# Four feed-forward gate/up groups as seven block products each, with the weight sums made on VectorE and by accumulating DMAs

## The chip, the cores and the metric

The kernel runs on one core of a Trainium2 chip. The metric is the device time of one execution in microseconds (us). Before the change it is 411.26 us, the median of 3 runs (410.68 to 411.28).

The engines are named as the profile names them: PE (TensorE, the matrix engine, with PEld its weight loads), DVE (VectorE), ACT (ScalarE), POOL (GpSimd) and SP (SyncE, which here only issues DMAs). A name with a q (SPq, POOLq) is the sequencer of that engine.

## The reference

One decoder layer on 256 tokens of width 1024, in float32: a token mixer (block-sparse attention and retention), a cross-attention into 256 memory rows, and a gated feed-forward part. The change lies in the last of these:

```python
h = rms_norm(x, g_pre_ffn[l])
gu = h @ w_gate_up[l]                                  # 1024 -> 2 * 2816
f = (jax.nn.silu(gu[..., :D_FF]) * gu[..., D_FF:]) @ w_down[l]
x = x + rms_norm(f, g_post_ffn[l])
```

`rms_norm(x, g)` scales each token's row by the inverse root of its mean square and each column by the gain `g`. `D_FF` is 2816, 22 tiles of 128 columns.

## The kernel before

All weights stand in DRAM as 130 blocks of 128 x 1024 floats, in the order of their use. Each goes through three stages.

- **Load.** SP's queue loads block q into one of 5 raw tiles (`load_weight`, L128), as soon as a raw tile is free.
- **Split.** `split_weight` makes two halves of it in one of 9 `hl` tiles (`RING`): ACT copies the block, rounded to the matmul's float32r type, into the high half (L136), and DVE subtracts that from the raw tile into the low half (L138). For 12 blocks of the feed-forward part (`POOL_LOW`) POOL does the subtraction.
- **Use.** A product of two split operands is three matmuls: high by high, high by low, low by high. The dropped term is low by low.

What PE does is a list of steps, built once; a step works on one block. Three of its forms matter here.

- **col** (L858 to L860): 128 tokens are stationary, 512 weight columns move; six matmuls of 512 columns for a block and a token half.
- **row** (L872, L874): a 128 x 128 weight tile is stationary and the tokens move. One matmul takes the 256 tokens' high and low halves side by side (512 columns) and a second one the high half against the weights' low half (256 columns). Eight such pairs make one tile of 128 gate or up columns for all tokens, already transposed.
- **down** (L892 to L894): as col, with the gated result as stationary operand, into four PSUM accumulators that stay open to the end.

The feed-forward part has six groups of gate and up columns. Group 0 (512 gate and 512 up columns) is in col form, first for tokens 0 to 127, then for 128 to 255, so that its 8 blocks are held through two passes; its result is transposed on PE (`c_f`, L501). Groups 1 to 4 (four gate and four up tiles each) and group 5 (two and two) are in row form; ACT, DVE and ACT again add the two halves of each accumulator, scale by the token's inverse root (a row `R_x2`, since tokens lie along the free axis), apply silu and multiply (L513 to L530). The down steps of a group stand behind the row steps of the next one.

The order of everything else is fixed by hand: what follows a step is a generator that is resumed a given number of steps later (the table `WAIT`), and splits are placed one per step, when the `hl` tile nine blocks back has been used. All instructions of an engine run in the order in which they were written down, and wait there for the tiles they need.

Ahead of the feed-forward part, `post_and_pre("cross", t)` adds the normalised output of the cross-attention to the 128 tokens of half t (L412), takes the mean square, and transposes x_sb on PE (`xt_cross`, L426); ACT and DVE scale it by the gain and split it into `x2T`. The inverse root is applied later, to gate and up.

Of the kernel before, what the change touches and what calls it, by code (L numbers as in the profile page):

```python
# [38 lines left out]
POOL_LOW = range(74, 122, 4)  # L39
# [5 lines left out]
def tile_hybrid_layer(  # L45
# [77 lines left out]
    raws, hls = {}, {}  # L123

    def load_weight(q):
        if q < NQ:
            raws[q] = rawp.tile([P, D], F32, tag="raw", name=f"raw{q}")
            nc.sync.dma_start(raws[q], weights[q])  # L128

    def split_weight(q, parts=1):  # L130
        raw = raws.pop(q)
        h = hlp.tile([P, 2, D], F32R, tag="hl", name=f"hl{q}")
        w = D // parts
        for i in range(parts):
            n = slice(i * w, (i + 1) * w)
            nc.scalar.activation(h[:, 0, n], raw[:, n], AF.Copy)  # L136
            eng = nc.gpsimd if q in POOL_LOW else nc.vector
            eng.tensor_tensor(out=h[:, 1, n], in0=raw[:, n], in1=h[:, 0, n].bitcast(F32), op=ALU.subtract)  # L138
# [25 lines left out]
    def split4(name, k0, t, c, n=4):  # L164
        dst = T[name][:, 0] if name == "fT" else T[name]
# [3 lines left out]
        emitted.update((name, k, t) for k in range(k0, k0 + n))  # L169
# [244 lines left out]
    def post_and_pre(stage, t, g, dst_name, key):  # L414
# [6 lines left out]
        dst = T[dst_name]  # L421
        for half in range(2):
# [72 lines left out]
    def ffn_up(t, acc):  # L495
        f = tmp2k(f"f0_{t}")
        nc.vector.scalar_tensor_tensor(f, acc, rstd[f"x2{t}"][:, 0:1], T[f"sg0_{t}"], op0=ALU.mult, op1=ALU.mult)
        yield WAIT[f"f0_{t}"]
        c = accC(f"c_f0_{t}")
        for i in range(4):  # L500
            nc.tensor.transpose(c[:, i, :], f[:, i * P:(i + 1) * P], ident)  # L501
        split4("fT", 0, t, c)

    def ffn_gate(t, acc):
        sg = tmp2k(f"sg0_{t}")
        nc.scalar.activation(sg, acc, AF.Silu, scale=rstd[f"x2{t}"][:, 0:1])
        T[f"sg0_{t}"] = sg

    def ffn_gate_T(i, acc):
# [6 lines left out]
        nc.vector.tensor_tensor(out=sg, in0=sg, in1=T["R_x2"], op=ALU.mult)  # L516
        yield WAIT["g_silu"]
        nc.scalar.activation(sg, sg, AF.Silu)  # L518
        yield WAIT["g_row"]
# [109 lines left out]

    def col_steps(order, tiles, done, st, skip=0):  # L630
# [4 lines left out]
        base = nq[0]  # L635
        nq[0] += len(order)
# [62 lines left out]
    def down_steps(js, tiles):
        blocks = [(j, kk) for j in js for kk in range(4 if j < 5 else 2)]  # L700
        base = nq[0]
        nq[0] += len(blocks)
        for ts in tiles:
            for i, (j, kk) in enumerate(blocks):
                for t in ts:
                    steps.append(("down", base + i, t, j, kk, (0, 1)))

    col_steps(plain([0, 1]), first_then, gu_first, "x2T")
    for j in range(1, 5):
        gu_steps(range(4 * j, 4 * j + 4))  # L710
        if j < 4:
            down_steps([j - 1], both)
    down_steps([3], both)
    gu_steps((20, 21))
    down_steps([4, 5], [(0,)])
    blocks_base = nq[0] - 6
    for half in range(2):
        for i in range(6):
# [299 lines left out]
```

## Time and profile before

| | us |
|---|---|
| median of the runs | 411.26 |
| span of the profiled execution, first to last instruction | 409.1 |
| PE busy | 401.2 |
| DVE busy | 290.9 |
| ACT busy | 237.5 |
| POOL busy | 42.5 |
| feed-forward groups' matmuls in row form, summed durations | 102.2 + 81.0 |

The mean granted clock of PE is 0.995 of full speed. Matmuls are pipelined, so their durations overlap and their sum says more than the time they take; the distance from the start of one to the start of the next is what they cost. DVE's and ACT's instructions overlap a little too, by less than 0.1 us.

The profiled execution's own time is its span, 409.1 us, and what lies around it: the median of the runs is 2.16 us above the span.

### The profile page before, as it was taken

Reading aid. Unit: us, or ns where it says so; the run is one execution under the profiler, and the core shown is the slowest. Engines: PE = TensorE matmul, PEld = TensorE weight load, DVE = VectorE, ACT = ScalarE, POOL = GpSimd, SP = SyncE. Lnnn points to the kernel's source line nnn. Section 1 sums busy time; section 2 is a strip of 40 time slices with the busy share of each in tenths; the row PEclk is TensorE's granted clock in tenths of the full one; section 3 lists DMA queues with packets and bytes.
Section 4 is the critical chain, followed back from the end, with each engine's and each line's share of the span. In section 5 each row is a group of like instructions: output and inputs, shape, how many; then the busy total and the mean of one; then the engine's idle time right before and its main releaser. Section 6 shows DMA issues by size and latency. Waiting matters only on the chain.

```text
span 409.1 us, 5760 instructions
## 1 busy us (share of the span) xinstructions
PE 401.2 (98%) x2114; PEld 336.9 (82%) x2114; DVE 290.9 (71%) x444; ACT 237.5 (58%) x438; POOL 42.5 (10%) x33
## 2 busy tenths in 40 slices
PE   8999999999999999999999999999999999999993
PEld 4888787888888888888888888888888888888882
DVE  4876975765889966678359577777878687777632
ACT  4887785945776763686158566374454545555411
POOL 0010100100010000000011031222222222200000
PEclk9999999999999999999999999999999999999997
DMA  7988654475656565147306756458457447456001
GB/s 264 410 346 286 229 187 167 147 259 181 208 184 199 190 211 166 49 158 256 105 14 209 265 183 205 154 172 291 123 189 256 155 154 269 143 154 207 1 27 75
DMA packets 21627, 76.17 MB, mean 186 GB/s; under 512 B 2400, under 2 KB 2656, under 8 KB 21600
## 3 DMA queue, kind: packets, MB, share of 16 engines
q1 hardware_dynamic: 21456, 75.56, 54.4%
q8 instruction: 16, 0.26, 0.3%
q10 hardware_dynamic: 144, 0.26, 0.2%
q14 instruction: 11, 0.09, 0.1%
HBM read 74.76 MB, written 1.05 MB: 185 GB/s over the span
## 4 chain that ended last, share of the span: by engine, by line
PE 94%; issue 2%; DMA 1%; ACT 0%; SPq 0%; DVE 0%; DVEq 0%; POOLq 0%; POOL 0%; ACTq 0%
PE acc L872 24%; PE acc L874 12%; PE acc L858 12%; PE acc L860 12%; PE acc L859 12%; PE down L892 4%; PE down L894 4%; PE down L893 4%; PE acc L845 2%; DMA raw<-in_weights_dram 1%; PE s_m L277 1%; PE o_m L306 1%; PE pt_m L256 1%; PE ro L359 0%; PE s_c L446 0%
## 5 line engine op out<-in xcount | busy, mean ns | idle before, releaser
L138 DVE TENSOR_TENSOR hl<-raw,hl 128x1024 fp32r<-128x1024 f32 (+1 forms) x120 | 147.2, 1251 | 41.2 <-ACT hl L136 36.4
L136 ACT ACTIVATE hl<-raw 128x1024 fp32r<-128x1024 f32 (+1 forms) x132 | 132.5, 1037 | 7.9 <-DMA raw<-in_weights_dram 6.2
L872 PE MATMUL acc<-x2T,hl 128*128 128x512 f32 x288 | 102.2, 399 | 0.0
L874 PE MATMUL acc<-x2T,hl 128*128 128x256 f32 x288 | 81.0, 281 | 0.0
L872 PEld LDWEIGHTS acc<-x2T,hl 128*128 128x128 f32 x288 | 54.2, 188 | 13.3
L874 PEld LDWEIGHTS acc<-x2T,hl 128*128 128x128 f32 x288 | 54.5, 189 | 0.2
L138 POOL TENSOR_TENSOR hl<-raw,hl 128x1024 fp32r<-128x1024 f32 x12 | 30.7, 2556 | 100.6 <-ACT hl L136 80.7
L892 PE MATMUL down<-hl,fT 128*128 128x512 f32 x88 | 34.3, 390 | 0.0
L893 PE MATMUL down<-hl,fT 128*128 128x512 f32 x88 | 34.3, 390 | 0.0
L894 PE MATMUL down<-hl,fT 128*128 128x512 f32 x88 | 34.3, 390 | 0.0
L858 PE MATMUL acc<-hl,xT 128*128 128x512 f32 x80 | 32.7, 409 | 0.0
L860 PE MATMUL acc<-hl,xT 128*128 128x512 f32 x80 | 31.4, 392 | 0.0
L859 PE MATMUL acc<-hl,xT 128*128 128x512 f32 x80 | 31.2, 390 | 0.0
L449 ACT ACTIVATE fT<-sg 128x256 fp32r<-128x256 f32 x18 | 7.5, 418 | 29.4 <-DVE sg L530 29.3
L872 PE MATMUL acc<-memT,hl 128*128 128x512 f32 x64 | 22.9, 400 | 0.0
L872 PE MATMUL acc<-x1T,hl 128*128 128x512 f32 x64 | 22.7, 399 | 0.0
L530 DVE TENSOR_TENSOR sg<-sg 128x256 f32<-128x256 f32 x18 | 20.1, 1118 | 0.6
L518 ACT ACTIVATE sg<-sg 128x256 f32<-128x256 f32 x18 | 7.5, 418 | 22.0 <-DVE sg L516 22.0
L894 PEld LDWEIGHTS down<-hl,fT 128*128 128x128 f32 x88 | 16.5, 188 | 3.5
L892 PEld LDWEIGHTS down<-hl,fT 128*128 128x128 f32 x88 | 16.5, 188 | 3.5
L893 PEld LDWEIGHTS down<-hl,fT 128*128 128x128 f32 x88 | 16.5, 188 | 3.3
L874 PE MATMUL acc<-x1T,hl 128*128 128x256 f32 x64 | 18.0, 281 | 0.0
(210 smaller groups left out, 724.8 us busy)
## 6 DMA issues: line engine op xcount, KB each, us to landing
raw<-in_weights_dram SPq DMA_DIRECT2D x129, 512.0 KB, 4.3
gpost<-in_gpost_dram SPq DMA_DIRECT2D x3, 512.0 KB, 5.2
x_sb<-in_x_dram SPq DMA_DIRECT2D x2, 512.0 KB, 6.9
memn<-in_mem_dram SPq DMA_DIRECT2D x2, 512.0 KB, 6.4
mr<-in_memT_dram SPq DMA_DIRECT2D x2, 512.0 KB, 5.1
out_dram<-x_sb SPq DMA_DIRECT2D x4, 256.0 KB, 2.0
xr<-in_gx_dram SPq DMA_DIRECT2D x1, 512.0 KB, 8.7
cst<-in_consts_dram SPq DMA_DIRECT2D x1, 512.0 KB, 7.6
```

Source lines behind the costliest of these rows:

```text
L136: nc.scalar.activation(h[:, 0, n], raw[:, n], AF.Copy)
L138: eng.tensor_tensor(out=h[:, 1, n], in0=raw[:, n], in1=h[:, 0, n].bitcast(F32), op=ALU.subtract)
L530: nc.vector.tensor_tensor(out=f, in0=f, in1=buf[:, 0:256], op=ALU.mult)
L845: nc.tensor.matmul(accs[(c, t)], T["xT"][:, hx, 2 * kp + kk, tok(t)], h[:, hw, :], start=begin, stop=False)
L858: nc.tensor.matmul(acc, xh, h[:, 0, kk, :], start=(first and kk == 0), stop=False)
L859: nc.tensor.matmul(acc, xh, h[:, 1, kk, :], start=False, stop=False)
L860: nc.tensor.matmul(acc, xl, h[:, 0, kk, :], start=False, stop=(last and kk == 1))
L872: nc.tensor.matmul(acc.rearrange("p (s m) -> p s m", s=2), hls[q][:, 0, n], T[st][:, :, k, :], start=(k == 0), stop=False, skip_group_chec ...
L874: nc.tensor.matmul(acc[:, 0:256], hls[q][:, 1, n], T[st][:, 0, k, :], start=False, stop=(k == 7), skip_group_check=True)
L892: nc.tensor.matmul(acc, fh, wh, start=first, stop=False, skip_group_check=True)
L893: nc.tensor.matmul(acc, fh, wl, start=False, stop=False, skip_group_check=True)
L894: nc.tensor.matmul(acc, fl, wh, start=False, stop=last, skip_group_check=True)
```

## The change

**Block products.** For groups 1 to 4, gate and up are computed together in col form as one product of 2 x 2 blocks: rows are the two token halves, the inner dimension is the two halves of the width, columns are 512 gate columns and 512 up columns. With A the tokens and B the weights, eight products of blocks are replaced by seven (`P1` to `P7`), each of 12 matmuls with 128 x 512 moving columns:

- P1 = A11 B11, P2 = A12 B21, P5 = S1 (B11 + B12), P6 = S2 (B11 + B12 + B22), P3 = S4 B22, P7 = S3 (B22 + B12), P4 = A22 (B11 + B12 + B21 + B22),
- with S1 = A21 - A22, S2 = S1 - A11, S3 = A11 - A21, S4 = S2 + A12.

P1, P6, P7 and P4 add up in one PSUM bank (`bA`), P5 and P3 in another (`bC`), P2 has a third (`bG`). Between the products ACT copies the bank's state (P1, P5, P1 + P6) and DVE combines (gate of half 0 = P1 + P2; up of half 0 = P5 + P3 less P1 + P6; up of half 1 = P5 less P1 + P6 + P7; gate of half 1 is the bank after P4).

**Sums of weights.** Raw tiles now serve several splits. DVE adds one raw tile to another in place (L195 of the new kernel; P6 and P4: 16 sums), and after the splits of P1 and of P3 a DMA on POOL's queue adds block B12 from DRAM onto the raw tile (L198; 16 DMAs). Each product has its own split: 14 per group where there were 8. There are 122 blocks loaded by SP. POOL no longer makes low halves. Raw tiles are 8 from the cross-attention on, and five idle buffers of other pools serve as raw tiles too.

**Tokens.** The inverse root and the gain are applied before the transposes (`y`), ACT keeps an unsplit copy (`af`), and DVE forms S1 to S4 and their low halves (`sh`, `sl`) once. The row `R_x2` goes. The gated result of groups 1 to 4 is token-major and is transposed on PE like that of group 0 (`ffn_mult`). Group 5 stays in row form and moves ahead into group 1. Down blocks are interleaved with the products (`ffn_plan`). The waits of steps around this part are set anew, and in the feed-forward part up to two splits are placed per step.

On PE, where group 1 begins: before, the pairs of the row form (`acc146` is a gate tile, `hl72` its split block);

```order
L860 MATMUL acc142_2319<-hl71_2198,x2T_1949 128x512
L872 MATMUL acc146_2361<-x2T_1949,hl72_2209 128x512
L874 MATMUL acc146_2361<-x2T_1949,hl72_2209 128x256
L872 MATMUL acc146_2361<-x2T_1949,hl72_2209 128x512
L874 MATMUL acc146_2361<-x2T_1949,hl72_2209 128x256
```

and now, between P5 (`bC1`) and P6 (`bA1`) of group 1, with the transposes of group 0's result:

```order
L1071 MATMUL bC1_2425<-hl77_2359,sh_2308 128x512
L1072 MATMUL bC1_2425<-hl77_2359,sh_2308 128x512
L1073 MATMUL bC1_2425<-hl77_2359,sl_2309 128x512
L1071 MATMUL bA1_2370<-hl80_2401,sh_2308 128x512
L1072 MATMUL bA1_2370<-hl80_2401,sh_2308 128x512
...
L1073 MATMUL bA1_2370<-hl80_2401,sl_2309 128x512
L622 MATMUL c_f0_1_2451<-cst_93,sg0_1_2326 128x128 x4
L1071 MATMUL bA1_2370<-hl81_2417,sh_2308 128x512
```

The pairs of 512 and 256 columns have become triples of 512; tile 80 is used ahead of 78 and 79, which belong to P3.

On DVE, at the same place, before:

```order
L497 SCALAR_TENSOR_TENSOR f0_0_2280<-acc134_2250,r_x20_2070,sg0_0_2220 128x512
L138 TENSOR_TENSOR hl73_2301<-raw73_2119,hl73_2301 128x1024
L138 TENSOR_TENSOR hl75_2326<-raw75_2184,hl75_2326 128x1024
L138 TENSOR_TENSOR hl76_2337<-raw76_2201,hl76_2337 128x1024
L138 TENSOR_TENSOR hl77_2348<-raw77_2212,hl77_2348 128x1024
L497 SCALAR_TENSOR_TENSOR f0_1_2359<-acc142_2319,r_x21_2196,sg0_1_2312 128x512
```

and now, from the split of P5's second block on (`hl77`; `raw72` and `raw73` are the two B11 blocks of group 1, `raw76` and `raw77` its B22 blocks):

```order
L184 TENSOR_TENSOR hl77_2359<-raw73_2071,hl77_2359 128x1024
L195 TENSOR_TENSOR raw72_1977<-raw72_1977,raw76_2122 128x1024
L618 TENSOR_TENSOR sg0_1_2326<-acc142_2334,sg0_1_2326 128x512
L184 TENSOR_TENSOR hl78_2377<-raw76_2122,hl78_2377 128x1024
L195 TENSOR_TENSOR raw73_2071<-raw73_2071,raw77_2151 128x1024
L184 TENSOR_TENSOR hl79_2397<-raw77_2151,hl79_2397 128x1024
L184 TENSOR_TENSOR hl80_2401<-raw72_1977,hl80_2401 128x1024
L230 TENSOR_TENSOR fT_2176<-c_f0_0_2410,fT_2176 128x4x128
L184 TENSOR_TENSOR hl81_2417<-raw73_2071,hl81_2417 128x1024
```

Ahead of these rows stand, new too, the splits 73 to 76 and, between 74 and 75, the eight instructions of 128 x 512 that form S1 to S4 and their low halves.

On POOL, before the first of the feed-forward part's low halves and now the first accumulating DMAs:

```order
L150 TENSOR_TENSOR r_x21_2196<-v_x21_2194,mhalf_99 128x1
L138 TENSOR_TENSOR hl74_2314<-raw74_2171,hl74_2314 128x1024
L138 TENSOR_TENSOR hl78_2377<-raw78_2304,hl78_2377 128x1024
L138 TENSOR_TENSOR hl82_2492<-raw82_2351,hl82_2492 128x1024
L138 TENSOR_TENSOR hl86_2601<-raw86_2469,hl86_2601 128x1024
```

```order
L210 TENSOR_TENSOR r_x21_2218<-v_x21_2216,mhalf_99 128x1
L198 DMA raw72_1977<-in_weights_dram 128x1024
L198 DMA raw73_2071<-in_weights_dram 128x1024
L198 DMA raw76_2122<-in_weights_dram 128x1024
L198 DMA raw77_2151<-in_weights_dram 128x1024
```

POOL's instructions on tiles have become DMAs on its queue; `raw73`, written by the second of them, is read again by the split `hl77` above.

The core of the diff:

```diff
 RING = 9
-RAW = 5
+RAW = 8
-POOL_LOW = range(74, 122, 4)
+PRODUCTS = {
+    "P1": ("A", "A11"), "P2": ("G", "A12"), "P5": ("C", "S1"), "P6": ("A", "S2"),
+    "P3": ("C", "S4"), "P7": ("A", "S3"), "P4": ("A", "A22"),
+}
+CHAIN = {
+    "P1": ("b11", None, "b12", ()), "P2": ("b21", None, None, ()), "P5": ("b11", None, None, ()),
+    "P3": ("b22", None, "b12", ()), "P6": ("b11", "b22", None, ()), "P4": ("b11", "b21", None, ("b11", "b21")),
+    "P7": ("b22", None, None, ("b22",)),
+}
...
+    pe = [(1, "P1 P2 P5 P6 r P3 r P1+ r P7 r P4 d"), (2, "P2 d P5 P6 d P3 d P1+ d P7 d P4"),
+          (3, "P2 d P5 P6 d P3 d P1+ d P7 d P4"), (4, "P2 d P5 P6 d P3 d d P7 d P4 d")]
+    prep = [(1, "P1 P2 P5 P3 P6 r r P1+ r P4 P7 r d"), (2, "P2 d P5 P3 P6 d d P1+ d P4 P7 d"),
+            (3, "P2 d P5 P3 P6 d d P1+ d P4 P7 d"), (4, "P2 d P5 P3 P6 d d P4 d P7 d d d d d d d")]
...
+    def split_weight(h, parts=1):
+
+        kind, q, add, more, frees = preps[h]
+        raw = raws[q][0]
+        split_raw(h, raw, parts)
+        while added[0] < min(len(preps), h + 1 + WAIT["ahead"]):
+            q, add = preps[added[0]][1:3]
+            if add is not None:
+                nc.vector.tensor_tensor(out=raws[q][0], in0=raws[q][0], in1=raws[add][0], op=ALU.add)
+            added[0] += 1
+        if more is not None:
+            nc.gpsimd.dma_start(raw, weights[more], accum_op=ALU.add)
+        for r in frees:
+            release(r)
...
+    def ffn_tokens(t, dst):
+        ys = []
+        for half in range(2):
+            n = slice(half * 512, (half + 1) * 512)
+            y = tmp2k(f"y{t}{half}")
+            nc.vector.scalar_tensor_tensor(y, x_sb[:, t, n], rstd[f"x2{t}"][:, 0:1], T["gpre"][:, n], op0=ALU.mult,
+                                           op1=ALU.mult)
+            ys.append(y)
...
+    def ffn_mult(j, t, up, wait):
+
+        f = T.pop(f"sg{j}_{t}")
+        nc.vector.tensor_tensor(out=f, in0=up, in1=f, op=ALU.mult)
+        yield wait
+        c = accC(f"c_f{j}_{t}")
+        for i in range(4):
+            nc.tensor.transpose(c[:, i, :], f[:, i * P:(i + 1) * P], ident)
+        split4("fT", 4 * j, t, c)
...
+        elif s[0] == "str":
+            _, q, j, prod, b = s
...
+            for kk in range(2):
+                ah, al = token_form(form, 2 * b + kk)
+                nc.tensor.matmul(acc, ah, h[:, 0, kk, :], start=first and kk == 0, stop=False, skip_group_check=True)
+                nc.tensor.matmul(acc, ah, h[:, 1, kk, :], start=False, stop=False, skip_group_check=True)
+                nc.tensor.matmul(acc, al, h[:, 0, kk, :], start=False, stop=b == 1 and kk == 1, skip_group_check=True)
...
-        if pending_split:
+        for n in range(2):
+            if not pending_split:
+                break
             q = pending_split[0]
-            paced = q <= 2 + WAIT["pace"] * 0.01 * i
-            free = q < RING or last_use[q - RING] + WAIT["lag"] <= i
-            if paced and free and (quiet or q - s[1] <= WAIT["low"]):
-                split_weight(pending_split.pop(0), 2 if q < 4 else 1)
+            if not all(last_use[h] + WAIT["lag"] <= i for h in range(q - RING + 1)):
+                break
+            if q < ffn_prep:
+                go = n == 0 and q <= 2 + WAIT["pace"] * 0.01 * i and (quiet or q - s[1] <= WAIT["low"])
+            else:
+                lead = first_use[q] - i
+                go = lead <= (WAIT["flow"] if n or not quiet else WAIT["flead"])
+            if not go:
+                break
+            split_weight(pending_split.pop(0), 2 if q < 4 else 1)
```

In `CHAIN` a product names the block it splits, the block that DVE adds to it first, the block that a DMA adds afterwards, and the blocks it frees. In the plan, a letter r stands for a row tile of group 5, d for a down block, and P1+ for P1 of the next group.

More of the change, by code (lines that the diff above doesn't have):

```diff
@@ L628, in tile_hybrid_layer, with plain_blocks @@
     nq = [0]
+    def plain_blocks(n):
+        h = len(preps)
+        for _ in range(n):
+            preps.append(("plain", nq[0], None, None, (nq[0],)))
+            loads.append(nq[0])
+            nq[0] += 1
+        return h
     def col_steps(order, tiles, done, st, skip=0):
@@ L649, in row_steps @@
         for i in tiles:
+            h = plain_blocks(1)
             for half in range(2):
-                steps.append(("row", nq[0], half, st, i, done))
-            nq[0] += 1
+                steps.append(("row", h, half, st, i, done))
     def plain(chunks):
@@ L688, in gu_first @@
         if c == 0:
-            ffn_gate(t, acc)
-        else:
-            spawn(ffn_up(t, acc))
+            sg = tmp2k(f"sg0_{t}")
+            nc.scalar.activation(sg, acc, AF.Silu)
+            T[f"sg0_{t}"] = sg
+        else:
+            spawn(ffn_mult(0, t, acc, WAIT[f"f0_{t}"]))
+    col_steps(plain([0, 1]), first_then, gu_first, "x2T")
+    pe_order, prep_order, load_order, extra = ffn_plan()
+    block = {k: nq[0] + n for n, k in enumerate(load_order + extra)}
+    loads.extend(range(nq[0], nq[0] + len(load_order)))
@@ L693, in gu_done @@
+    at = {}
+    ffn_prep = len(preps)
+    for item in prep_order:
+        at[item] = len(preps)
+        if item[0] in CHAIN:
+            src, add, more, frees = CHAIN[item[0]]
+            src, add, more = (n and block[(n, *item[1:])] for n in (src, add, more))
+            preps.append((item, src, add, more, tuple(block[(n, *item[1:])] for n in frees)))
+        else:
+            preps.append((item, block[item], None, None, (block[item],)))
     def gu_done(i, acc):
         return ffn_up_T(i - 100, acc) if i >= 100 else ffn_gate_T(i, acc)
-    def gu_steps(tiles):
-        row_steps([i + up for i in tiles for up in (0, 100)], gu_done, "x2T")
@@ L699, in down_steps @@
[L699 to L716, printed above, removed]
+    for item in pe_order:
+        if item[0] in CHAIN:
+            steps.append(("str", at[item], item[1], item[0], item[2]))
+        elif item[0] == "row":
+            for half in range(2):
+                steps.append(("row", at[item], half, "x2T", item[1], gu_done))
+        else:
+            for t in range(2):
+                steps.append(("down", at[item], t, item[1] // 4, item[1] % 4, (0, 1)))
@@ L717, in tile_hybrid_layer @@
+    tail = [(k, at[item]) for item in prep_order if item[0] == "down" and item not in pe_order for k in item[1:]]
+    for k, h in tail:
+        steps.append(("down", h, 0, k // 4, k % 4, (0, 1)))
     for half in range(2):
-        for i in range(6):
-            j, kk = (4, i) if i < 4 else (5, i - 4)
-            steps.append(("down", blocks_base + i, 1, j, kk, (half,)))
-    assert nq[0] == NQ, nq[0]
+        for k, h in tail:
+            steps.append(("down", h, 1, k // 4, k % 4, (half,)))
@@ L723, in tile_hybrid_layer, with raw_tile @@
     last_use = {s[1]: i for i, s in enumerate(steps)}
+    first_use = {s[1]: i for i, s in reversed(list(enumerate(steps)))}
     nc.vector.memset(junk[:, 0:512], 0.0)
     nc.gpsimd.memset(mhalf, -0.5)
-    raws[0] = rawp.tile([P, D], F32, tag="raw", name="raw0")
-    nc.scalar.dma_start(raws[0][:, 0:512], weights[0, :, 0:512])
+    def raw_tile():
+        q = loads.pop(0)
+        raw_free["raw"] -= 1
+        raws[q] = (rawp.tile([P, D], F32, tag="raw", name=f"raw{q}"), "raw")
+        return raws[q][0]
```

231 lines of the change are left out of this document (174 added, 57 removed), and 16 rows, old and new, of the table WAIT.

## The prediction

> **What bounds the kernel now.** I read the page's busy times and its chain of waits first, then the granted clock and engine loads by windows, then TensorE's (PE's) instructions one by one.
>
> ```profile
> span 409.1 us, 5760 instructions
> PE 401.2 (98%) x2114; PEld 336.9 (82%) x2114; DVE 290.9 (71%) x444; ACT 237.5 (58%) x438; POOL 42.5 (10%) x33
> PE 94%; issue 2%; DMA 1%; ACT 0%; SPq 0%; DVE 0%; DVEq 0%; POOLq 0%; POOL 0%; ACTq 0%
> ...
> 15.00:110.00 95.00, 95.00 (x519) 77.26 (x519) 70.72 (x110) 68.88 (x136) 5.14 (x6) 1.00 0.66 231
> ...
> 265.00:290.00 25.00, 25.00 (x131) 21.32 (x130) 20.14 (x25) 13.27 (x20) 7.81 (x3) 1.00 0.65 214
> 290.00:315.00 25.00, 25.00 (x129) 21.25 (x129) 18.83 (x26) 13.51 (x22) 5.41 (x2) 1.00 0.60 204
> ```
>
> The chain that ended last is PE for 94%, and no window between 15 and 390 us has idle time on PE (the first busy figure equals the window) at a granted clock of 1.00. So an instruction taken from PE shortens the run by its pitch, as long as its suppliers keep up. The nearest supplier is VectorE (DVE), which in the feed-forward windows works 20.1 and 18.8 us of 25.
>
> The mean durations on the page (399 ns for a 128x512 matmul) overlap. What counts is the distance from start to start:
>
> ```profile
> 261.63 0.40 PE L872 MATMUL acc<-x2T,hl 128*128 128x512 f32 x1
> 261.86 0.28 PE L874 MATMUL acc<-x2T,hl 128*128 128x256 f32 x1
> ...
> 263.75 0.39 PE L892 MATMUL down<-hl,fT 128*128 128x512 f32 x1
> ...
> 267.86 0.39 PE L892 MATMUL down<-hl,fT 128*128 128x512 f32 x1
> ```
>
> ```profile
> 242.04 0.48 PE L872 MATMUL acc<-x2T,hl 128*128 128x512 f32 x1
> 242.35 0.28 PE L874 MATMUL acc<-x2T,hl 128*128 128x256 f32 x1
> ```
>
> ```profile
> 241.84 0.44 PE c_f L501 x4
> ```
>
> The first two fences are the timeline of PE (start, duration), the third a piece of the chain (start, length). Six pairs L872+L874 take 263.75 - 261.63 = 2.12 us, 0.353 us a pair; the eighteen matmuls from 263.75 to 267.86 take 4.11 us, 0.228 us each. Four 128x128 transposes take 0.44 us.
>
> **The change on PE.** L872 and L874 are the weight-stationary form (a tile of 128 gate or up columns, eight pairs each); of the 36 feed-forward tiles in these groups 32 go:
>
> ```profile
> L872 PE MATMUL acc<-x2T,hl 128*128 128x512 f32 x288 | 102.2, 399 | 0.0
> L874 PE MATMUL acc<-x2T,hl 128*128 128x256 f32 x288 | 81.0, 281 | 0.0
> ```
>
> Removed: 256 pairs x 0.353 = 90.4 us, and the two transposes of the row norm with what follows them, 0.2. Added: 4 groups x 7 products x 12 matmuls of 512 columns = 336 x 0.228 = 76.6 us. Eight products a group in the new form would be 87.6 us, so 2.8 us come from leaving the pair form and 11.0 from the missing product. Added too: the gated result of each group is now token-major and is transposed, 32 transposes x 0.11 = 3.5 us, in 8 batches; the first matmul behind a batch holds PE 0.31 us instead of 0.23 (242.04 to 242.35), 0.6 in all. Down products (264 matmuls) and the first group stay. Net 90.6 - 76.6 - 3.5 - 0.6 = **9.9 us less PE**, if PE never waits.
>
> **The change on DVE.** Uncontended prices, and the pitch when splits follow each other:
>
> ```profile
> L138 DVE TENSOR_TENSOR hl<-raw,hl 128x1024 fp32r<-128x1024 f32 x22 | 26.2, 1221 | 4.2 <-ACT hl L136 4.2
> L248 DVE TENSOR_TENSOR p_m<-p_m,rs_m 128x1024 f32<-128x1024 f32 x3 | 3.7, 1225 | 0.1
> L405 DVE TENSOR_TENSOR cg_mix<-acc,gpost 128x512 f32<-128x512 f32 x4 | 2.7, 687 | 2.2 <-ACT junk L155 2.2
> L450 DVE TENSOR_TENSOR fT<-sg,fT 128x256 fp32r<-128x256 f32 x18 | 7.6, 422 | 3.9 <-ACT fT L449 3.9
> L136 ACT ACTIVATE hl<-raw 128x1024 fp32r<-128x1024 f32 x126 | 129.1, 1056 | 5.8 <-DMA raw<-in_weights_dram 4.2 <-PE acc L860 1.6
> ```
>
> ```profile
> 211.71 3.50 DVE L138 TENSOR_TENSOR hl<-raw,hl 128x1024 fp32r<-128x1024 f32 x3 [0.80 <-ACT hl L136]
> ```
>
> These are groups of instructions by line and shape (count, busy us and mean ns, idle us before them and its releaser; the first between 140 and 215 us, where POOL has no split), then a row of DVE's timeline. Pitch of a 128x1024 instruction: (3.50 - 1.22) / 2 = 1.14 us, 0.08 under its duration; the same taken off gives 0.61 for 512 columns and 0.34 for 256. An in-place weight sum has the shape of L248 (1.225), so 1.14 too. A middle group (from its P2 to the next P2) holds on DVE 19 splits, 4 sums and 7 instructions of 512: 23 x 1.14 + 7 x 0.61 = 30.5 us. PE in the same stretch: 7 x 12 + 5 down blocks x 12 = 144 matmuls x 0.228 + 0.88 + 0.16 = 33.9 us. DVE is at 90% where it was at about 80%: enough, but a DVE that falls behind regains only 3.4 us per group.
>
> Nine split tiles exist, so DVE cannot work ahead freely. The tightest place is before group 1. The eight tiles of the first group are held through two passes, so the split of tile 73 waits for the second pass's first step. From there to the second matmul of P6 (tile 80) PE has 7 x 6 + 36 matmuls and a batch of transposes, 18.3 us. DVE has splits 73 to 80, two sums, eight instructions for the token sums and one gating product: 10 x 1.14 + 9 x 0.61 = 16.9 us, plus 1.2 until ScalarE's first high half is there (L136, 1.06, and the hand-over), plus about 0.8 where the token sums wait for each other or for ScalarE: 18.9. I charge **1.0 us** of PE waiting for tiles 80 to 82 (bounds 0 and 3: nothing waits, or each of the eight token instructions comes 0.22 later still, as L450 waits for ScalarE 3.9 us over 18).
>
> The POOL split goes, and with it its collisions:
>
> ```profile
> 300.78 2.56 POOL L138 TENSOR_TENSOR hl<-raw,hl 128x1024 fp32r<-128x1024 f32 x1 [10.83 <-ACT hl L136]
> ...
> 301.45 2.17 DVE L530 TENSOR_TENSOR sg<-sg 128x256 f32<-128x256 f32 x1
> ```
>
> L530 takes 0.42 elsewhere and 2.17 here, beside POOL. That is DVE time that is not in the 30.5 us.
>
> **From cross-attention to the feed-forward.** The normalised rows are now formed before they are transposed.
>
> ```profile
> 205.78 0.23 PE acc L858
> ```
>
> ```profile
> 207.21 0.20 DVE L148 TENSOR_SCALAR v_p_cross<-ss_cross 128x1 f32<-128x1 f32 x1
> 208.07 1.41 DVE L412 SCALAR_TENSOR_TENSOR x_sb<-cg_cross,r_p_cross,x_sb 128x512 f32<-128x512 f32 x2 [0.67 <-POOL r_p_cross L150]
> 210.76 0.15 DVE L146 TENSOR_SCALAR v_x<-ssx_cross 128x1 f32<-128x1 f32 x1 [1.28 <-ACT junk L155]
> ```
>
> Tokens 0 to 127 leave PE at 205.8 and x_sb is done at 209.48. Behind it now stand two splits (2 x 1.14 = 2.3, longer than the 1.28 that DVE waited for the mean square), the inverse root (0.86, as from v_p_cross to L412: 208.07 - 207.21), v_x (0.15) and one half row (1.41 / 2 = 0.7): ready at 213.5. The transposes stand six steps of six matmuls behind 205.8, at 214.0. The cover is 0.5 us; I charge 0.3, and 0.75 more if a split is late.
>
> **The accumulating DMAs.** Sixteen DMAs of 512 KB from POOL's queue add weights onto a tile that has just been split. No row of before shows one. The nearest:
>
> ```profile
> raw<-in_weights_dram SPq DMA_DIRECT2D x129, 512.0 KB, 4.3
> xr<-in_gx_dram SPq DMA_DIRECT2D x1, 512.0 KB, 8.7
> ```
>
> Below: a plain load, 4.3 us. Above: twice the slowest load, 17.4, as it must read the tile too. I take twice the usual one, 8.6, since queues are at half load in these windows. What hides it: between the split that releases a tile and the split that reads it again stand 16 to 19 us of DVE work everywhere but once. In group 1, from split 73 to ScalarE's part of split 77, stand split 74, eight token sums and two high halves, 8 us. So the cost is 8.6 - 8 = **0.6 us**, then at DVE, and behind the waiting ScalarE instruction the high halves of 78 to 80. POOL has nothing behind these DMAs until the last norm.
>
> The Trainium skill ("DMA: Bandwidth & Descriptors", "Anatomy of one DMA — SWDGE (gpsimd) path") fits a DMA from GpSimd as 2.0 us plus bytes over 436 GB/s; that is an estimate of 3.2 us here, and by it the sum below is 0.6 lower. No run here shows it yet.
>
> **Loads and the end.** SP's loads grow by 8 net with the accumulated ones counted, 4 MB on 76, at half-busy queues and 13 buffers for raw tiles, each load issued some ten splits (over 11 us) ahead of a 4.3 us landing: nothing. The last steps after PE are the same instructions as before.
>
> **Sum:** 409.1 - 9.9 + 1.0 + 0.3 + 0.6 = 401.1 us of span. The median of the runs before, 411.26, is 2.16 above the span of its profile; I keep that difference: **403.3 us**.
>
> **Rivals.**
> 1. *PE never waits.* 409.1 - 9.9 + 2.16 = 401.4. For it: PE had no idle window in before with the same nine tiles. Against it: the 18.9 against 18.3 us.
> 2. *DVE late in every group.* The late start of group 1 is not regained and each group pays another 1 to 1.5 us where sums, high halves and splits wait in turn: 403.3 + 4 x 1.25 less what tile 80 already paid, 407 or so. For it: from the previous P4's end, which frees a split tile, to P6 of groups 3 and 4 PE has P2, a down block, P5 and two batches of transposes, 36 x 0.228 + 1.06 = 9.3 us; DVE has two sums, the splits 117 to 119 and two 512s, 5 x 1.14 + 2 x 0.61 = 6.9 us, and ScalarE's transposed copy, its silu and first high half stand before them. Some 1.5 us are left.
> 3. *DVE becomes the bound: slower than before.* In before, DVE stood idle before its splits:
>
> ```profile
> L138 DVE TENSOR_TENSOR hl<-raw,hl 128x1024 fp32r<-128x1024 f32 x44 | 59.7, 1377 | 26.8 <-ACT hl L136 22.1 <-PE acc L860 4.4
> ```
>
> That is 0.61 us for each of 44 splits between 240 and 390 us, mostly for ScalarE. If this is latency that stays and not slack, a group costs 30.5 + 23 x 0.61 = 44.5 us against 33.9; already 0.3 us each makes 37.4, 3.5 over PE, 14 us in four groups: 415. It decides from 0.25 us on (36.2 a group, the gain gone). Against it: DVE ran three splits at 1.14 in a row, and ScalarE is only 53% busy.
> 4. *Slow accumulation: slower too.* Above some 17 us a DMA costs 9 at tile 77 and begins to show in the other groups: about 412 at 17 us, 417 at 20. For it speaks how POOL's work fares beside DVE's splits:
>
> ```profile
> 211.00 0.55 POOL L150 TENSOR_TENSOR r_x<-v_x,mhalf 128x1 f32<-128x1 f32 x1 [2.96 <-DVE v_x L146]
> 224.32 1.46 POOL L150 TENSOR_TENSOR r_x<-v_x,mhalf 128x1 f32<-128x1 f32 x1 [3.86 <-DVE v_x L146]
> ```
>
> The second ran beside a split and took 0.9 longer; a POOL that has to get past ten splits for one DMA would be 9 us late. The Trainium skill ("SBUF — State Buffer", "SBUF: two separate sides") says why that may be: POOL and DVE take turns at a shared port pair, and DVE's two-port modes keep POOL from writing DMA descriptors; but it limits the block by DVE instructions with two SBUF inputs, as the splits are, to POOL instructions that read SBUF, which would speak for my price.
>
> **Chances.** My forecast, with 402 to 405: 0.50. Rival 1: 0.15. Rival 2 (405 to 410): 0.20. Rival 3: 0.08. Rival 4: 0.07. The range is 400.8 to 409.5: it takes in rivals 1 and 2 nearly whole and leaves out 3 and 4 and a little of each end. A change below 0.2% (0.8 us) can't be told from none. Faster 0.85, no difference 0.03, slower 0.12.
>
> **What would show it.** PE's matmuls at 0.228 in the new products, 336 of them; PE idle, if anywhere, before P6 of group 1, released by DVE's split; DVE busy over 85% between groups 1 and 4; accumulating DMAs landing in 5 to 12 us and no ScalarE wait on them beyond tile 77. I am wrong if PE waits in every group, or if the DMAs from POOL take 15 us or more.

## The result

The changed kernel takes **401.72 us** (median; 401.39 to 401.97) against 411.25 (410.68 to 411.28) for the kernel before in the same runs: a ratio of 0.977, 95% interval 0.9756 to 0.9784. The forecast was 403.3 with a range of 400.8 to 409.5, so the sign and the range held, and the forecast itself was 1.6 us too high. Rival 1 (401.4) came nearer, though its condition, that PE never waits, is not quite met.

The page of the changed kernel: span and busy times, the queue of the accumulating DMAs, the chain of waits, two groups of instructions (POOL's accumulating DMAs and DVE's sums), and the weight loads by queue (count, size, median us from issue to landing).

```profile
span 399.6 us, 5462 instructions
PE 391.1 (98%) x1968; PEld 324.1 (81%) x1968; DVE 312.5 (78%) x424; ACT 255.9 (64%) x421; POOL 25.1 (6%) x37
...
q0 software_dynamic: 2304, 8.39, 11.9%
...
PE 90%; DVE 3%; issue 2%; ACT 1%; DMA 1%; SPq 0%; DVEq 0%; POOLq 0%; POOL 0%; ACTq 0%
...
L198 POOL DMA_DIRECT2D raw<-in_weights_dram x16 | 14.2, 885 | 113.8 <-DVE hl L184 104.9
L195 DVE TENSOR_TENSOR raw<-raw,raw 128x1024 f32<-128x1024 f32 x16 | 19.5, 1217 | 0.0
...
raw<-in_weights_dram SPq DMA_DIRECT2D x121, 512.0 KB, 5.4
raw<-in_weights_dram POOLq DMA_DIRECT2D x16, 512.0 KB, 6.3
```

The span fell by 9.5 us (409.1 to 399.6). PE is still 90% of the chain, and nearly all of DVE's 3% has a single place. The windows:

```profile
15.00:240.00 225.00, 225.00 (x1219) 189.09 (x1218) 168.34 (x267) 150.01 (x286) 11.47 (x16) 1.00 0.63 214
240.00:390.00 150.00, 149.29 (x691) 123.51 (x690) 133.71 (x139) 96.40 (x120) 12.79 (x15) 1.00 0.62 179
...
240.00:290.00 50.00, 49.29 (x238) 40.77 (x237) 49.59 (x54) 36.87 (x48) 5.24 (x6) 1.00 0.70 193
290.00:380.00 90.00, 90.00 (x408) 74.52 (x407) 79.73 (x79) 57.55 (x67) 7.00 (x8) 1.00 0.64 191
```

From 15 to 390 us PE (first pair of figures after the window's length) is idle for 0.7 us, all of it between 240 and 290. DVE (third pair) is busy for 49.59 of 50 us there, and for 89% of the 90 us behind. PE's timeline shows the place:

```profile
248.64 0.39 PE L1071 MATMUL bA<-hl,sh 128*128 128x512 f32 x1
249.74 0.50 PE L1072 MATMUL bA<-hl,sh 128*128 128x512 f32 x1 [0.71 <-DVE hl L184]
250.08 0.39 PE L1073 MATMUL bA<-hl,sl 128*128 128x512 f32 x1
```

It is the second matmul of P6 in group 1, released by DVE's split: the place that the prediction had named. From start to start it is 1.10 us where 0.23 is usual, a loss of 0.87. How the wait came about stands on ScalarE's and DVE's timelines:

```profile
230.67 1.06 ACT L183 ACTIVATE hl<-raw 128x1024 fp32r<-128x1024 f32 x1 [0.29 <-PE acc L1042]
```

```profile
247.34 2.35 DVE L184 TENSOR_TENSOR hl<-raw,hl 128x1024 fp32r<-128x1024 f32 x2
```

The first row is the high half of tile 73, held up until PE's second pass over group 0 has used the first of its tiles; the second holds the splits of tiles 79 and 80, done at 249.69 (247.34 + 2.35). That is 19.0 us from 230.67, where the prediction had worked out 18.9.

### The profile page after: what moved, and what is told of

It reads as the page before. It is cut to its first block, busy times and chain, and to the rows that moved or that the text cites. A ratio compares the mean times of both kernels' runs of the same rounds, so it can differ in the third digit from the quotient of the medians.

```text
span 399.6 us, 5462 instructions
## 1 busy us (share of the span) xinstructions
PE 391.1 (98%) x1968; PEld 324.1 (81%) x1968; DVE 312.5 (78%) x424; ACT 255.9 (64%) x421; POOL 25.1 (6%) x37
## 3 DMA queue, kind: packets, MB, share of 16 engines
HBM read 79.48 MB, written 1.05 MB: 202 GB/s over the span
## 4 chain that ended last, share of the span: by engine, by line
PE 90%; DVE 3%; issue 2%; ACT 1%; DMA 1%; SPq 0%; DVEq 0%; POOLq 0%; POOL 0%; ACTq 0%
PE acc L1040 11%; PE acc L1042 11%; PE acc L1041 11%; PE acc L1054 9%; PE acc L1056 5%; PE down L1092 4%; PE down L1090 4%; PE down L1091 4%; PE bA L1072 3%; PE bA L1073 3%; PE bA L1071 3%; PE acc L1027 2%; PE bC L1073 2%; PE bC L1071 2%; PE bC L1072 2%
## 5 line engine op out<-in xcount | busy, mean ns | idle before, releaser
L184 DVE TENSOR_TENSOR hl<-raw,hl 128x1024 fp32r<-128x1024 f32 (+1 forms) x156 | 181.5, 1198 | 18.6 <-ACT hl L183 17.9
L183 ACT ACTIVATE hl<-raw 128x1024 fp32r<-128x1024 f32 (+1 forms) x156 | 155.3, 1040 | 12.6 <-DVE raw L195 6.4
L1090 PE MATMUL down<-hl,fT 128*128 128x512 f32 x80 | 31.5, 394 | 0.0
L1092 PE MATMUL down<-hl,fT 128*128 128x512 f32 x80 | 31.2, 390 | 0.0
L1091 PE MATMUL down<-hl,fT 128*128 128x512 f32 x80 | 31.2, 389 | 0.0
L198 POOL DMA_DIRECT2D raw<-in_weights_dram x16 | 14.2, 885 | 113.8 <-DVE hl L184 104.9
L195 DVE TENSOR_TENSOR raw<-raw,raw 128x1024 f32<-128x1024 f32 x16 | 19.5, 1217 | 0.0
L229 ACT ACTIVATE fT<-c_f 128x512 fp32r<-128x512 f32 x10 | 6.0, 597 | 20.2 <-PE c_f L622 20.2
L1056 PE MATMUL acc<-memT,hl 128*128 128x256 f32 x64 | 18.0, 281 | 0.0
L1042 PEld LDWEIGHTS acc<-hl,xT 128*128 128x128 f32 x80 | 15.0, 188 | 3.3
L1092 PEld LDWEIGHTS down<-hl,fT 128*128 128x128 f32 x80 | 15.0, 188 | 3.2
L1040 PEld LDWEIGHTS acc<-hl,xT 128*128 128x128 f32 x80 | 15.0, 188 | 3.1 <-issue 0.3
L1091 PEld LDWEIGHTS down<-hl,fT 128*128 128x128 f32 x80 | 15.0, 188 | 3.0
L1090 PEld LDWEIGHTS down<-hl,fT 128*128 128x128 f32 x80 | 15.0, 188 | 3.0
L1041 PEld LDWEIGHTS acc<-hl,xT 128*128 128x128 f32 x80 | 15.1, 189 | 2.7
L1054 PEld LDWEIGHTS acc<-x1T,hl 128*128 128x128 f32 x64 | 12.0, 188 | 3.0
## 6 DMA issues: line engine op xcount, KB each, us to landing
gpost<-in_gpost_dram SPq DMA_DIRECT2D x3, 512.0 KB, 10.1
x_sb<-in_x_dram SPq DMA_DIRECT2D x2, 512.0 KB, 10.1
```

The lines of the kernel that those rows point to most:

```text
L183: nc.scalar.activation(t[:, 0, n], raw[:, n], AF.Copy)
L184: nc.vector.tensor_tensor(out=t[:, 1, n], in0=raw[:, n], in1=t[:, 0, n].bitcast(F32), op=ALU.subtract)
L1040: nc.tensor.matmul(acc, xh, h[:, 0, kk, :], start=(first and kk == 0), stop=False)
L1041: nc.tensor.matmul(acc, xh, h[:, 1, kk, :], start=False, stop=False)
L1042: nc.tensor.matmul(acc, xl, h[:, 0, kk, :], start=False, stop=(last and kk == 1))
L1054: nc.tensor.matmul(acc.rearrange("p (s m) -> p s m", s=2), hls[q][:, 0, n], T[st][:, :, k, :], start=(k == 0), stop=False, skip_group_chec ...
```

## The experiments

### What the missing product is worth

The changed kernel with eight products a group in the same form:

```diff
-    pe = [(1, "P1 P2 P5 P6 r P3 r P1+ r P7 r P4 d"), ...
+    pe = [(1, "g0 g1 g2 g3 r u0 u1 r u2 u3 r r d"), ...
+            for t in range(2):
+                steps.append(("col", at[item], t, "x2T", 2 * second + item[2], ...
```

> Groups 1 to 4 in the changed kernel's col form and token-major result, but as eight block products: no sums of weights, no sums of tokens, no accumulating DMAs, eight splits a group. Theory (the saved time is the missing product): 4 x 12 matmuls x 0.228 = 10.9 us more on TensorE than in the changed kernel, less the 0.8 us that it waits before P6 of group 1, which has nothing to wait for here: 401.7 + 10.1 = 411.8 us, that is, no faster than before (the 2.8 us from leaving the pair form are spent on the 4.1 us of transposes). Rival (the gain comes from the form, the new order or POOL's splits going): 402 to 406 us.

412.17 us (411.42 to 412.54), 1.0016 of the kernel before (1.0006 to 1.0026), so the new form with all eight products is slightly slower than the old kernel. That is 10.4 us above the changed kernel where 10.1 was expected, and the rival is out: the order, the form and POOL's relief together do not make the kernel faster. The gain is the missing product. (POOL's relief alone is worth about 0.5 us, as the last experiment shows; the form costs more than that.)

### The wait before P6 of group 1

First VectorE's sums were left out:

```diff
-            if add is not None:
+            if False:
                 nc.vector.tensor_tensor(out=raws[q][0], in0=raws[q][0], in1=raws[add][0], op=ALU.add)
```

> VectorE's 16 in-place sums of weights are left out (the products P6 and P4 then take wrong weights; every split, DMA and matmul stays). Theory (VectorE has spare time in groups 2 to 4 and is late only before P6 of group 1): 16 x 1.14 = 18.2 us less VectorE work, and the time falls by just the 0.8 us of that wait, to 400.9 us. Rival (VectorE is the hidden bound of the groups, by its waits in turn with ScalarE): several us less, 396 to 399. If nothing waited for VectorE at all: 401.7.

Products P6 and P4 then take weights without their sums; every split, DMA and matmul stays. 400.46 us (400.19 to 400.65); the span is 398.8, 0.8 below the changed kernel's, and the times differ by 1.3 in the medians. In its windows PE never waits:

```profile
240.00:390.00 150.00, 150.00 (x695) 124.42 (x694) 116.75 (x123) 96.50 (x123) 12.79 (x15) 1.00 0.61 181
```

17 us less DVE work (133.71 to 116.75) bought, in the profiled executions, what the one wait cost (0.87) and nothing more: in the other groups the sums lie under PE. What the other 0.4 us between the medians are, the profiles do not show.

Then the order of the splits was changed so that P6's come ahead of P3's, which PE uses later:

```diff
-    prep = [(1, "P1 P2 P5 P3 P6 r r P1+ r P4 P7 r d"),
+    prep = [(1, "P1 P2 P5 P6 P3 r r P1+ r P4 P7 r d"),
```

> Only the order in which group 1's tiles are split changes: P6's two splits (and their two sums) ahead of P3's. Theory (TensorE's only wait, 0.8 us before P6 of group 1, is VectorE's queue: P3's two splits stand ahead of P6's although P3 is used after it): the wait goes, 0.7 to 0.9 us less, 400.9 us. Rival (the wait is the latency of ScalarE's first high half, or moves to P3): within 0.3 us of 401.7.

404.98 us (403.39 to 406.13), slower by 3.3. A new wait, before P5, on PE's timeline of the profiled execution (403.39 us, a span of 401.6):

```profile
245.36 0.60 PE L622 MATMUL c_f<-cst,sg 128*128 128x128 f32 x4
248.85 0.47 PE L1071 MATMUL bC<-hl,sh 128*128 128x512 f32 x1 [2.89 <-ACT hl L183]
```

The sums run three splits ahead. With P6 right behind P5 each of its two sums came to stand ahead of P5's own split of that tile, ScalarE had to wait for both (2.4 and 2.5 us), and sum, high half and low half ran in single file (P5 there takes sums in place of its weights; the amount of work is the same). The wait of 2.89 less the 0.87 that went make the 2.0 us by which this span is longer than the changed kernel's. The next kernel put the sums behind P5's splits:

```diff
-        while added[0] < min(len(preps), h + 1 + WAIT["ahead"]):
+        while added[0] < min(len(preps), h + 1 + (2 if kind[:2] in (("P2", 1), ("P5", 1)) else WAIT["ahead"])):
```

> Group 1's splits of P6 stand ahead of P3's, as in the kernel before this one, but now the two sums for P6 stay behind the splits of P5 that read the same raw tiles (there they had been placed ahead of P5's second split, which so took a wrong weight, and ScalarE waited for them). Theory (the wait before P6 of group 1 is VectorE's queue, with P3's two splits, 2.3 us, ahead of work that is used sooner): the wait of 0.8 us goes and nothing takes its place: 400.9 us, and no idle time on TensorE between 15 and 390 us. Rival (ScalarE's high halves or the sums' wait for P5's splits end last there): 401.4 to 402.5.

401.33 us (401.19 to 401.55), a ratio of 0.9755 (0.974 to 0.9769), which can't be told from the changed kernel's 0.977. The wait has moved:

```profile
246.94 0.47 PE L1071 MATMUL bC<-hl,sh 128*128 128x512 f32 x1 [0.65 <-DVE sg L618]
```

P5 now waits for the gating product of group 0, which stands behind both sums. The last of this series put one sum behind that product (the `2` above becomes 1 at P5's second split).

> As the kernel before this one (P6's splits ahead of P3's in group 1), but the second sum now stands behind the gating product of group 0 (L618) and behind P6's first split. In the kernel before, TensorE's wait had moved to P5 of group 1, 0.65 us, which writes the PSUM bank that this product reads, and the product stood behind both sums. Theory (the wait follows whatever stands last in VectorE's queue there, and the queue has room once the order fits the use): no wait on TensorE between 15 and 390 us, span 398.9 to 399.1, time 400.7 to 401.0. Rival (VectorE's work up to that point is too much in any order): a wait of about 0.7 us appears at another place, 401.4 to 401.8.

402.95 us (402.78 to 403.41), slower. PE's waits between 200 and 395 us (us in total, times, longest), and the reason on DVE's timeline:

```profile
PE c_f L622 <- DVE fT L230: 1.2, 1, 1.2
PE bA L1071 <- ACT p L630: 0.4, 1, 0.4
```

```profile
246.73 1.22 DVE L195 TENSOR_TENSOR raw<-raw,raw 128x1024 f32<-128x1024 f32 x1
249.15 1.23 DVE L184 TENSOR_TENSOR hl<-raw,hl 128x1024 fp32r<-128x1024 f32 x1 [1.21 <-ACT hl L183]
```

A sum directly ahead of the split of the same tile made DVE idle for 1.2 us here, since ScalarE's high half has to come between. The theories of the order fell, and so did the rival's 401.4 to 401.8 for this last one: no order that I tried fits all uses, the wait only changes its place, and what takes it away is less DVE work (the kernel without sums).

### How much time VectorE has to spare

Two, then four more VectorE instructions a group were added in groups 2 to 4, one behind each split of P3's tiles, and for four one behind each split of P1's too (the diff is that of two). P1 of group 2 is split ahead of P2 of group 2, so two of the twelve instructions stand there:

```diff
+        if kind[0] == "P3" and kind[1] > 1:
+            nc.vector.tensor_tensor(out=extra_dve, in0=raw, in1=hls[h][:, 0, :].bitcast(F32), op=ALU.subtract)
```

> Two more VectorE instructions of 128x1024 a group in groups 2 to 4 (their result is used nowhere), 2.3 us a group. Theory (VectorE has some 3 us to spare in each group, as 30.5 of 33.9 us says and as it is 91% busy between 290 and 365 us, and its waits are slack): they fit, 401.7 to 402.4 us. Rival (VectorE and ScalarE wait in turn, so that spare time can't be used): each is paid for, 3 x 2.3 = 6.9 us, 408.6.

> Four more VectorE instructions of 128x1024 a group in groups 2 to 4 (result unused), 4.6 us a group. Theory (3.1 to 3.4 us to spare a group): VectorE becomes the bound, 1.2 to 1.5 us a group are paid, and TensorE waits before P6 in groups 3 and 4: 403.5 to 406.5 us. Rival one (all of it is paid): 3 x 4.6 = 13.8, 415.5. Rival two (far more spare time than I worked out): 401.7 to 402.4.

404.81 us (404.46 to 405.22) and 411.41 (410.93 to 411.98): of 6.9 us added 3.1 were paid, of 13.8 added 9.7. Both lie between the theory and its rival, so the spare time that can be used is real but much smaller than worked out. The timelines of the kernel with four, ScalarE's and DVE's between 290 and 300 us, show one reason:

```profile
297.08 0.68 DVE L637 TENSOR_TENSOR p<-bG,p 128x512 f32<-128x512 f32 x1
299.90 1.22 DVE L185 TENSOR_TENSOR hl<-raw,hl 128x1024 fp32r<-128x1024 f32 x1 [2.13 <-ACT hl L184]
```

```profile
297.80 0.63 ACT L639 ACTIVATE p<-p 128x512 f32<-128x512 f32 x1 [7.60 <-DVE p L637]
298.34 0.58 ACT L646 ACTIVATE u<-bA 128x512 f32<-128x512 f32 x1
298.81 2.95 ACT L184 ACTIVATE hl<-raw 128x1024 fp32r<-128x1024 f32 x3
```

ScalarE stands 7.6 us before the silu of P2's result, for which DVE has not yet added P1 and P2. The high half that DVE needs next stands behind that silu in ScalarE's queue. So DVE, itself late, is idle for 2.1 us more. To test it, the silu was put behind two more high halves:

```diff
             nc.vector.tensor_tensor(out=p1, in0=bank["G"], in1=p1, op=ALU.add)
-            yield 1
+            yield 4
             nc.scalar.activation(p1, p1, AF.Silu)
```

> The kernel with four more VectorE instructions a group in groups 2 to 4 (411.4 us), and ScalarE's silu of P2 (L639 there) placed behind two more high halves instead of ahead of them. Theory (of the 3.4 us of spare time a group, 2.1 could not be used, since ScalarE waits for VectorE's sum with bG at this silu, up to 7.6 us, while the next high half, for which VectorE then waits 2.1 us, stands behind it): the 2.1 us come back in each of three groups, VectorE's waits for high halves nearly vanish, 404.5 to 406 us. Rival (the idle time is VectorE's own, by raw tiles or PSUM banks that come free late): 411, with the idle time at another place.

408.08 us (407.7 to 408.16), 3.3 less. DVE's waits for high halves between 270 and 380 us (us in total, times, longest), first with the early silu, then with the late one:

```profile
DVE hl L185 <- ACT hl L184: 4.1, 3, 2.1
```

```profile
DVE hl L185 <- ACT hl L184: 0.5, 1, 0.5
```

The mechanism holds: 3.6 us of idle time gone, 3.3 back. My size was wrong, because only one of the three waits was 2.1 us long (I had charged each so). The expected 404.5 to 406 us were missed for that. What is left, 6.4 us, is DVE's work: between 290 and 380 us DVE is now busy for 88.96 of 90 us. Where the first matmuls of P2 in groups 2, 3 and 4 stand, in the changed kernel and under it in this one (count, durations, first to last start):

```profile
L1071 PE MATMUL bG<-hl,x2T x4: 389/389/389, 278.4 to 280.5; 128*128 128x512 f32 x4
L1071 PE MATMUL bG<-hl,x2T x4: 389/392/478, 311.9 to 314.1; 128*128 128x512 f32 x4
L1071 PE MATMUL bG<-hl,x2T x4: 389/392/478, 345.5 to 347.7; 128*128 128x512 f32 x4
```

```profile
L1074 PE MATMUL bG<-hl,x2T x4: 389/389/390, 280.6 to 282.6; 128*128 128x512 f32 x4
L1074 PE MATMUL bG<-hl,x2T x4: 389/392/479, 316.1 to 318.2; 128*128 128x512 f32 x4
L1074 PE MATMUL bG<-hl,x2T x4: 389/392/479, 351.1 to 353.2; 128*128 128x512 f32 x4
```

A group lasts 33.5 and 33.6 us in the changed kernel (PE was worked out at 33.9), and 35.5 and 35.0 with four more instructions (DVE was worked out at 30.5, and 4 x 1.14 more make 35.1). So the sums of both engines were right within some 1%. Of the 6.4 us, 3.4 were paid in these two groups (351.1 - 280.6 against 345.5 - 278.4), 2.2 before P2 of group 2, where two of the added instructions stand (2 x 1.14 = 2.3), and the rest behind. Up to P2 of group 2 DVE has no spare time at all in the changed kernel (49.59 of 50 us between 240 and 290): it is still making up for its late start in group 1.

The kernel with two more instructions has the same three waits (4.1 us, longest 2.1), and they are there in the changed kernel too (four, 4.9 us), where they cost PE nothing. That they are why two instructions were paid in part is argued from this, not shown: that kernel was not run with the late silu.

### The price of the accumulating DMAs

```diff
-            nc.gpsimd.dma_start(raw, weights[more], accum_op=ALU.add)
+            nc.gpsimd.dma_start(raw, weights[more])
```

> The 16 DMAs from POOL's queue copy block B12 instead of adding it (P5, P6, P7 and P4 then take wrong weights); order, sizes and waits are the same. It prices the accumulation: the changed kernel's 16 DMAs land 6.3 us (median) after issue, SP's plain loads 5.4. Theory (accumulation reads the tile as well, as I priced it at twice a load): 4.5 to 5.5 us here. Rival (the extra time is the path from POOL's queue, and the addition is free): 6.0 to 6.6. The kernel's time stays at 401.7 by both, as none of these DMAs is waited for.

The sixteen DMAs copy block B12 over the tile instead of adding it. 401.36 us (401.01 to 401.65), the same time. The page of this kernel:

```profile
L198 POOL DMA_DIRECT2D raw<-in_weights_dram x16 | 8.8, 549 | 118.7 <-DVE hl L184 109.1
...
raw<-in_weights_dram SPq DMA_DIRECT2D x121, 512.0 KB, 5.1
raw<-in_weights_dram POOLq DMA_DIRECT2D x16, 512.0 KB, 4.0
```

The accumulation costs 2.3 us of landing (6.3 against 4.0) and 0.34 us of issuing on POOL (885 against 549 ns); POOL's queue by itself is no slower than SP's. The theory's direction holds, with a price of 1.6 plain DMAs instead of the two that I took; the plain ones are faster than the expected 4.5 to 5.5.

Then each accumulating DMA was cut into four of 128 KB:

```diff
-            nc.gpsimd.dma_start(raw, weights[more], accum_op=ALU.add)
+            for n in range(4):
+                nc.gpsimd.dma_start(raw[:, 256 * n:256 * n + 256], weights[more, :, 256 * n:256 * n + 256], accum_op=ALU.add)
```

> Each accumulating DMA as four of 128 KB, issued one after the other by POOL (0.9 us each to issue, so that the last starts some 2.6 us later). Theory (the cover at tile 77 was 7.4 us, and the whole DMA landed after 6.7 there, so only 0.7 us were left): landing 8.5 to 9.5 us after the first issue, ScalarE waits 1 to 2 us before tile 77's high half, the time rises by that to 403 to 403.7 us; elsewhere covers of 16 us and more hide it. Rival one (small DMAs are issued and land as fast as one large one): 401.7. Rival two (POOL's issuing is held up by VectorE's splits, more with more DMAs): over 405.

402.56 us (401.98 to 403.08), a ratio of 0.9784 (0.9769 to 0.9798), whose interval overlaps the changed kernel's. POOL's and ScalarE's timelines at tile 77:

```profile
233.12 3.58 POOL L199 DMA_DIRECT2D raw<-in_weights_dram  x4 [1.89 <-DVE hl L184]
```

```profile
239.63 1.04 ACT L183 ACTIVATE hl<-raw 128x1024 fp32r<-128x1024 f32 x1
241.02 2.01 ACT L183 ACTIVATE hl<-raw 128x1024 fp32r<-128x1024 f32 x2 [0.35 <-DMA raw<-in_weights_dram]
```

The four take 3.58 us to issue, and ScalarE waits 0.35 us for the last, 7.9 us after the first issue (241.02 - 233.12). Free for it ScalarE was from 240.67 on (239.63 + 1.04), so the cover is 7.6 us. The whole DMA, issued at 233.30 in the changed kernel, landed after 6.7 us, as the list of DMAs of that stretch has it, and ScalarE ran on without a wait:

```profile
raw<-in_weights_dram POOLq DMA_DIRECT2D x1, 512.0 KB, 6.7
```

```profile
238.84 3.89 ACT L183 ACTIVATE hl<-raw 128x1024 fp32r<-128x1024 f32 x4
```

I expected a wait of 1 to 2 us, as I added the whole delay of the last issue to the landing; the four together were only 1.2 us later than the one. Rival two (POOL's issuing held up by the splits) is out: it takes 0.9 us an issue, while DVE splits almost without a break.

### Late silu without added work, and POOL's share

Both edits together (P6's splits first as in the last kernel of that series, and the late silu) on the changed kernel:

> The changed kernel with P6's splits ahead in group 1 and the later silu, no added work. Theory (VectorE's spare time in groups 2 to 4 is not on the path, so the later silu gains nothing; the other order takes away the 0.7 us wait): as the kernel with the other order alone, 400.7 to 401.0 us. Rival (the silu's place costs something in the groups even here): 0.3 us or more below that kernel.

403.17 us (402.44 to 403.19), as the other order alone (402.95), for which 400.7 to 401.0 had been expected too. The later silu gains nothing where PE is the bound; the order is the worse one. Last, the kernel before without POOL's low halves:

```diff
-POOL_LOW = range(74, 122, 4)
+POOL_LOW = ()
```

> The kernel before the change with the 12 low halves that POOL made given to VectorE. Theory (TensorE is the bound there and VectorE has the time: 12 x 1.14 = 13.7 us more over 150 us, less the time that its instructions lose beside POOL): 411.3 us, no difference. Rival (part of the gain was POOL's splits going): 410 or less. If VectorE is late without POOL: over 412.

410.84 us (410.1 to 411.26), 0.9989 of the kernel before (0.998 to 0.9998): 0.5 us less than expected. It is not PE's: the median span of the runs is 409.1 us in both kernels. What fell is the time around the span, from 2.2 to 2.3 us in every run of the kernel before to 1.7 to 1.8 us in each of the ten here. Only the twelve splits differ, so it goes with them; by what way, no run shows. All the other kernels of this document, in which POOL has no splits either, have 1.7 to 1.9. The windows of this kernel, and under them the one of the kernel before that shows the start:

```profile
0.00:15.00 15.00, 13.68 (x51) 8.89 (x52) 8.26 (x15) 8.92 (x16) 0.31 (x5) 1.00 0.89 326
15.00:240.00 225.00, 225.00 (x1220) 189.25 (x1219) 164.32 (x269) 148.79 (x290) 10.47 (x14) 1.00 0.58 195
240.00:390.00 150.00, 150.00 (x793) 128.25 (x792) 104.88 (x164) 77.86 (x126) 0.00 (x0) 1.00 0.55 176
```

```profile
0.00:15.00 15.00, 13.17 (x47) 8.74 (x48) 7.57 (x14) 7.95 (x13) 0.31 (x5) 1.00 0.87 313
```

The execution shown has a span of 408.3 us. At 15 us it is four matmuls (0.9 us) ahead, long before any POOL split, and PE is full in both behind that; so POOL's splits cost PE nothing. Of the kernels that leave nothing out, none is measurably faster than the changed one.

## Why the prediction held, point by point

- **PE's work, -9.9 us.** The kernel without sums, in which PE never waits, is 10.3 us of span below the kernel before. The term was right to 0.4 us, within what the start of a run varies (0.9 us above). Its two parts were tested by the eight products: the missing product is worth 10.4 us of time (10.1 worked out: 10.9 less the wait), and form and transposes cost 1.3 us of span (410.4 against 409.1) where 3.5 + 0.6 - 2.8 - 0.2 = 1.1 was worked out.
- **The wait at tiles 80 to 82, +1.0.** Right in place and cause, 0.87 in size. The balance of 18.9 against 18.3 us gave 0.6; the charge made of it, 1.0, was meant for tiles 80 to 82, but all of the 0.87 was lost at tile 80.
- **The transition, +0.3, and the accumulation, +0.6.** Neither cost anything: PE's window from 15 to 240 us is full, and ScalarE did not wait at tile 77. For the accumulation the price of 8.6 us was too high (6.7 at that place), and the cover of 8 nearly right (7.6). How much of the transition's cover was left was not tried.
- **The 2.16 us around the span.** This term was carried over from the kernel before, and it was mis-sized: in the four runs of the changed kernel it is 1.8. It goes with POOL's splits, as the kernel before without them shows.
- **So the 1.6 us are three mis-sized terms:** waits of 1.9 charged and 0.9 met, 0.35 us around the span, and PE's work 0.2 to 0.5 us larger than worked out (by the median span of the runs, 399.9, and by the profile's, 399.6). That rival 1's 401.4 came nearer is in part luck: its sum leaves out the wait of 0.87 that was met, and the two other terms made up for it.
- **The signs that the prediction named** were seen: PE idle only before P6 of group 1, released by DVE's split, DVE busy for 89% of the time between 240 and 390 us, and accumulating DMAs that landed after 5.4 to 10.1 us.
- **Rival 2** needed DVE to be late in every group. It is not, but the margin was less than the 3.4 us a group on which I relied: up to P2 of group 2 there is none, and behind that the place of the silu can take up to 2.1 us of it. **Rival 3's** mechanism, ScalarE's latency that stays when DVE is late, exists (4.1 us over three groups with four more instructions), at a tenth of the 14 us a group that it would have cost by the idle times of the kernel before. Nine tenths of those idle times were slack.
- **Rival 4** is out: POOL issued each accumulating DMA in 0.9 to 1.05 us beside a DVE that was almost always splitting. The Trainium skill ("DMA: Bandwidth & Descriptors", "Anatomy of one DMA — SWDGE (gpsimd) path") gives by its fit an estimate of 3.2 us for a DMA of this size; the plain one measured 4.0, and the accumulating one 6.3.

## What to carry to other kernels

Where one engine is full from end to end, an instruction taken from it is worth its pitch from start to start, and the price of the scheme that replaces it is read from the supplier's sum in the stage with the least head start, not from its mean load. Spare time on a supplier is not spare if an instruction of a third engine that waits for it stands ahead of one that feeds it. An in-place sum needs another job between it and the split of the same tile. And what lies around the span is a term of its own: here it moved by 0.4 us with the work that POOL no longer does.

## What was not expected of the hardware

POOL's low halves cost VectorE more than they saved it. The groups of VectorE's instructions between 240 and 390 us, first in the kernel before, then in the same kernel without POOL's splits:

```profile
L138 DVE TENSOR_TENSOR hl<-raw,hl 128x1024 fp32r<-128x1024 f32 x44 | 59.7, 1377 | 26.8 <-ACT hl L136 22.1 <-PE acc L860 4.4
L530 DVE TENSOR_TENSOR sg<-sg 128x256 f32<-128x256 f32 x18 | 20.1, 1118 | 0.6
L516 DVE TENSOR_TENSOR sg<-sg,R_x 128x256 f32<-128x256 f32 x18 | 9.2, 512 | 0.6
```

```profile
L138 DVE TENSOR_TENSOR hl<-raw,hl 128x1024 fp32r<-128x1024 f32 x53 | 63.8, 1222 | 21.3 <-ACT hl L136 20.9
L530 DVE TENSOR_TENSOR sg<-sg 128x256 f32<-128x256 f32 x18 | 7.7, 425 | 0.6
L516 DVE TENSOR_TENSOR sg<-sg,R_x 128x256 f32<-128x256 f32 x18 | 7.6, 425 | 0.6
```

With nine more splits of its own VectorE is busy for 104.88 us in that stretch; in the kernel before it was 114.13, as its window shows:

```profile
240.00:390.00 150.00, 150.00 (x794) 128.33 (x794) 114.13 (x155) 77.15 (x126) 28.26 (x11) 1.00 0.54 179
```

L530, which the prediction had shown at 2.17 us beside a POOL split, fell from 1118 to 425 ns in the mean. The time of the kernel shows none of this, since PE is full in both. The accumulating DMAs, which POOL issues, show no such effect: DVE's sums, of which that at 246.20 us runs beside an issue (246.58 to 247.45), all take 1214 to 1219 ns, as the same shape does elsewhere (1225).
